# The mLSTM gates' projection and their side work, moved behind the Fourier projection and spread over the jobs of the attention's values

## The chip, the cores and the metric

The kernel runs on one core of one Trainium2 chip. The metric is device time in microseconds (us) of one execution, as the median over runs. The engines are TensorE (PE: matmuls, with its weight loads as PEld), VectorE (DVE), ScalarE (ACT), GpSimd (POOL) and SyncE (SP, which here issues nearly all DMAs). In the profile L12 means line 12 of the kernel.

## The reference

The program is a trunk of two layers for 256 latent tokens and 256 context tokens of width 1024. In each layer the tokens are normalised and modulated (adaLN), and one input projection feeds three parallel branches, of which these columns matter here:

```python
u = h @ w_in                 # columns: mLSTM q, k, v, o; 16 gate columns; attention q, k, v; Fourier z; ...
i_f, f_f, i_b, f_b = split(u[gate columns] + gate_b, 4)      # 4 heads, forward and backward in time
b = cumsum(log_sigmoid(f))                                   # running sums and maxima of the mLSTM
m_t = maximum(b + m, max over s <= t of (b_t - b_s + i_s))
yd = differential attention with axial rotary of (dq, dk, dv)
yf = real part of a 2-D Fourier transform of z
```

A merge of the branches, a residual and a SwiGLU feed-forward follow. All is float32. The second layer needs the latent tokens' output only.

## The kernel before

A float32 product is made of three matmuls on operands split into a high and a low part: `proj_t` (L303 on) computes W^T h with the weights stationary, and per chunk of 128 rows of W it issues high x high (L310), high x low (L311) and low x high (L312). `proj_n` (L331 to L333) is the form with the tokens as rows. The weights come as *jobs*, one per block of W. A job is loaded by SP (`wr`, L204, 512 KB; four raw buffers), its high part `wh` is cast by ACT (L214, about 1.05 us), its low part `wl` is made by DVE (L224, about 1.25 us), and then its matmuls run. `run_all` writes the program job by job: it loads 7 jobs ahead and splits 3 ahead. Jobs of `proj_t` have 24 matmuls. A matmul over 512 tokens is issued every 0.23 us, one over 256 every 0.12 us.

Beside the jobs run *sides*: generators (`side(name, gen, steps, jobs)`) that are advanced one step at a time between pieces of the jobs, spread evenly over a stated number of jobs, and finished by `drain(name)`. SP keeps the program's order; the other engines' order is made by the scheduler of the framework from the program's order and the buffers that are free. PSUM has four main banks (`m`, the jobs' results) and four side banks (`p`).

One layer's attention and Fourier part runs, in the program's order, as follows. Four (layer 0) or three (layer 1) dk jobs run inside the opening of the layer, while the tokens are normalised. Then come the rest of the eight dk jobs, eight dq jobs (in layer 1 over the 256 latent tokens alone, like dq's matmuls there), the Fourier projection z (`proj_z`, eight jobs, folded weights: sums of two raw blocks made by DVE and POOL at L790, edges copied by ACT at L792; layer 0's matmuls are L813 to L815, layer 1's L817; at its end 32 or 16 small matmuls, L837), eight dv jobs, and then q, k, v of the mLSTM. Each dk or dq job ends in a rotary evacuation from its bank, four DVE products L1215, one L1216 and a POOL sum L1217. The dv jobs keep all four main banks for four jobs, and evacuate them by copies that DVE (L1362) and ACT share.

The gates' job (`GateJob`) is a `proj_t` job with 16 used columns: POOL clears its raw buffer (L231), SP loads it by four DMAs (L233), ACT casts it, and POOL, not DVE, makes the low part (L222). Its result stays in a side bank. `ml_gates` (L1003 to L1072) is its side work in 18 steps on 36 rows of 512: DVE copies the bank out (L1016, L1019), adds the bias (L1025), forms a log-sigmoid by a polynomial (twelve times L1033), a running sum (L1040) and a running maximum (L1045), copies the results with the backward half reversed (L1055, L1057); then PE transposes them eight times (L1062) and DVE takes the columns out (L1066). The mLSTM, far later, is the first to use them.

Two more sides matter: `adab` and `adac` compute rows of the modulation from w_ada (per step two DMAs of 512 KB at L365, and eight matmuls L372 in four column strips), and `hf` (`fold_h`, L751 to L774) folds the tokens for z on DVE.

Of the kernel before, what the change touches and what calls it, by code (L numbers as in the profile page):

```python
# [26 lines left out]
CQ, CK, CV, CO, CGATE, CDQ, CDK, CDV, CZ, CG = 0, 1024, 2048, 3072, 4096, 4112, 5136, 6160, 7184, 8208  # L27
# [16 lines left out]
def tile_trunk(ctx: ExitStack, tc: tile.TileContext, x, c, cx, c_ctx, w_ada, b_ada, norm_g, w_in, ml_gate_b,  # L44
# [30 lines left out]
    def main_ps():  # L75
        return pm.tile([128, 512], F32, tag="m", name=nm("m"))

    def side_ps():
        return psd.tile([128, 512], F32, tag="s", name=nm("p"))
# [105 lines left out]
    def act_k(acts, k, n0, n1):  # L185
        return acts[0][k // 2][:, k % 2, n0:n1], acts[1][k // 2][:, k % 2, n0:n1]

    def unit_n():
        return upool.tile([128, 4, 256], F32, tag="u4", name=nm("n"))
# [46 lines left out]
    def call(fn):  # L236
        prog.append(("call", fn))

    def side(name, gen, steps, jobs):
        prog.append(("side", name, gen, steps / (4.0 * jobs)))  # L240

    def drain(name):
        prog.append(("drain", name))
# [60 lines left out]
    def proj_t(src, acts, n0, evac, cls=Job):  # L304

        def run(job):
            ps = side_ps() if cls is GateJob else main_ps()
            for k in range(KB):
                ah, al = act_k(acts(), k, n0, NT)
                T.matmul(ps[:, n0:], lhsT=job.hi[:, k, :], rhs=ah, start=(k == 0), stop=False)  # L310
                T.matmul(ps[:, n0:], lhsT=job.hi[:, k, :], rhs=al, start=False, stop=False)  # L311
                T.matmul(ps[:, n0:], lhsT=job.lo[:, k, :], rhs=ah, start=False, stop=(k == KB - 1))  # L312
                if k == KB - 1:
                    evac(ps)
                if k % 2:
                    yield
        prog.append(cls(src, KB, 128, run))

    def proj_n(src, nk, acts, tbs, evac):

        st = {}

        def mk(kt):
            def run(job):
                if kt == 0:
                    st.update({tb: main_ps() for tb in tbs})
                for tb in tbs:
                    for j in range(2):
                        k = 2 * kt + j
                        ah, al = act_k(acts(), k, tb * 128, tb * 128 + 128)  # L330
                        T.matmul(st[tb], lhsT=ah, rhs=job.hi[:, j, :], start=(k == 0), stop=False)  # L331
                        T.matmul(st[tb], lhsT=ah, rhs=job.lo[:, j, :], start=False, stop=False)  # L332
                        T.matmul(st[tb], lhsT=al, rhs=job.hi[:, j, :], start=False, stop=(k == nk - 1))  # L333
                    if kt == nk // 2 - 1:
                        evac(tb, st[tb])
                    yield
            return run
        for kt in range(nk // 2):
            prog.append(Job(src[kt * 256:kt * 256 + 256, :], 2, 512, mk(kt)))
# [994 lines left out]
    def plan(l, xget, fin, bd1, bd2, bdn):  # L1334
# [6 lines left out]
        W = w_in[l]  # L1341
        vc = {n: vcol[:, 32 * l + o:32 * l + o + 8] for n, o in VROW.items()}
        st = {"yd": ([], []), "ym": ([], []), "q": [], "k": [], "v": [], "dq": [], "dk": [], "dv": [],
              "ys": [], "yy": ([], []), "us": ([], []), "ox": []}
# [14 lines left out]
        h = lambda: bd1().h  # L1359
# [17 lines left out]
        def proj_tt(key, c0, nn0, rot=False, b0=0):  # L1377
            for b in range(b0, 8):
                proj_t(W[:, c0 + b * 128:c0 + b * 128 + 128], h, nn0, evac_t(key, nn0, b, rot))

        def proj_nn(key, c0, tt, f):
            for g in range(2):
                def evac(tb, ps, g=g):
                    if tb == tt[0]:
                        st[key] += [unit_n(), unit_n()]
                    for j in range(2):
                        f(st[key][2 * g + j][:, tb, :], ps[:, j * 256:j * 256 + 256], j)
                proj_n(W[:, c0 + g * 512:c0 + g * 512 + 512], KB, h, tt, evac)
# [61 lines left out]
            opening_jobs(bd1, specs, parts)  # L1450
        else:
            first_jobs(bd1, specs)
        proj_t(W[:, CGATE:CGATE + 16], h, 0, lambda ps: st.__setitem__("gps", ps), GateJob)
        call(start)
        side("gates", lambda: ml_gates(l, st["gps"], st), 18, 10)
        side("adab", ada[1].steps, 10, 10)
        proj_tt("dk", CDK, 0, True, nop)
        side("hf", lambda: fold_h(h(), len(segs), hf, st), 12 if l == 0 else 8, 7 * nT // 4)
        proj_tt("dq", CDQ, n0, True)
        drain("gates")  # L1460
        drain("adab")
        drain("hf")
        proj_z(l, W, len(segs), hf, st)
        side("adac", ada[2].steps, 10, 8)
        proj_nn("dv", CDV, ALL, cp)
        drain("adac")
        qjobs = 8 * nT // 4
        side("da", lambda: diff_attn(l, st, tbs), (8 * nT + 4) * 3, qjobs + 15)
# [134 lines left out]
    ctx.enter_context(tc.manual_schedule(engines={mybir.EngineType.SP}))  # L1603
    call(begin)
    plan(0, None, fin, bd[0], bd[1], bd[2])
    plan(1, lambda: fin[0], fin, bd[2], bd[3], bd[4])
    run_all()

# [55 lines left out]
```

## Time and profile before

| | before |
|---|---|
| median of 3 runs | 2001.8 us (1996.95 to 2003.03) |
| the profiled execution | 1996.54 us, span 1994.5 us, mean granted clock 0.987 |
| PE busy | 1930.8 us, 97% of the span |
| DVE busy | 1192.4 us, 60% |
| ACT busy | 783.6 us, 39% |
| POOL busy | 148.1 us, 7% |

Times are in us from the span's start. [...] A row of the timeline gives an instruction's start and duration, and in brackets the idle time before it with what ended it. Matmuls are pipelined, so a row's duration (0.39 us for 512 columns) is longer than the distance to the next.

### The profile page before, as it was taken

To read this page: it belongs to the slowest core of one execution; us is meant where nothing else is said; L and a number is where in the kernel's file an instruction comes from. 1 tells how busy PE (TensorE), PEld (TensorE's weight loads), DVE (VectorE), ACT (ScalarE), POOL (GpSimd) and SP (SyncE) were. 2 spreads that over 40 slices of the span, in tenths; PEclk is the share of its full clock that TensorE was granted. 3 is DMA by queue.
4 is the path that set the end of the run, shared out by engine and by line. 5 is a ranking of instruction groups with operands and counts; after the bars stand their busy time and mean duration, and the time that the engine had idled before them with its cause. 6 is when DMAs were issued, how large, how long until landed. Compare 5 with 4: busy or idle time off the path is not lost.

```text
span 1994.5 us, 27678 instructions
## 1 busy us (share of the span) xinstructions
PE 1930.8 (97%) x10504; PEld 1591.5 (80%) x10504; DVE 1192.4 (60%) x2592; ACT 783.6 (39%) x1466; POOL 148.1 (7%) x164
## 2 busy tenths in 40 slices
PE   6999999999999999999999999989999999989998
PEld 4768687888777778888777888776878978879996
DVE  4895488852476457653333235982984486476655
ACT  3223376632344223352222224322773354235443
POOL 0240000000000110000000000250100010000000
PEclk8999999999999999999999999999999999899999
DMA  9547522224321333434443332668322654465663
GB/s 292 171 138 222 194 64 60 58 92 120 116 74 54 95 86 115 159 106 137 148 137 95 117 95 44 213 204 283 96 64 83 184 171 143 119 187 158 182 198 130
DMA packets 339895, 269.49 MB, mean 135 GB/s; under 512 B 17233, under 2 KB 296145, under 8 KB 339762
## 3 DMA queue, kind: packets, MB, share of 16 engines
q1 hardware_dynamic: 339040, 265.09, 43.9%
q10 hardware_dynamic: 722, 2.62, 0.3%
q8 instruction: 83, 1.36, 0.3%
q14 instruction: 50, 0.41, 0.1%
HBM read 264.73 MB, written 7.11 MB: 136 GB/s over the span
## 4 chain that ended last, share of the span: by engine, by line
PE 76%; DVE 14%; ACT 4%; DMA 3%; issue 2%; SPq 0%; POOL 0%; DVEq 0%; ACTq 0%; POOLq 0%
PE m L310 12%; PE m L312 12%; PE m L311 12%; PE m L331 6%; PE m L333 6%; PE m L332 6%; DVE wl L224 3%; PE p L1152 2%; DVE t L1215 2%; PE m L568 2%; PE m L566 2%; PE m L567 2%; PE p L372 1%; PE p L1116 1%; PE m L681 1%
## 5 line engine op out<-in xcount | busy, mean ns | idle before, releaser
L224 DVE TENSOR_TENSOR wl<-wr,wh 128x1024 fp32r<-128x1024 f32 x336 | 418.7, 1249 | 446.2 <-ACT wh L214 444.6
L214 ACT CAST wh<-wr 128x1024 fp32r<-128x1024 f32 x336 | 351.6, 1049 | 687.1 <-issue 265.3
L310 PE MATMUL m<-u,wh 128*128 128x512 f32 (+1 forms) x1752 | 616.3, 352 | 1.7 <-ACT wh L214 1.7
L312 PE MATMUL m<-u,wl 128*128 128x512 f32 (+1 forms) x1752 | 604.0, 345 | 1.6 <-DVE wl L224 1.6
L311 PE MATMUL m<-u,wh 128*128 128x512 f32 (+1 forms) x1752 | 602.9, 344 | 0.0
L310 PEld LDWEIGHTS m<-u,wh 128*128 128x128 f32 x1752 | 334.2, 191 | 63.2 <-issue 13.8
L312 PEld LDWEIGHTS m<-u,wl 128*128 128x128 f32 x1752 | 333.8, 191 | 41.5 <-DVE wl L224 2.7
L311 PEld LDWEIGHTS m<-u,wh 128*128 128x128 f32 x1752 | 334.1, 191 | 38.8 <-issue 3.2
L331 PE MATMUL m<-wh,u 128*128 128x512 f32 x532 | 216.3, 407 | 0.0
L333 PE MATMUL m<-wh,u 128*128 128x512 f32 x532 | 208.4, 392 | 0.0
L332 PE MATMUL m<-wl,u 128*128 128x512 f32 x532 | 207.9, 391 | 0.0
L331 PEld LDWEIGHTS m<-wh,u 128*128 128x128 f32 x532 | 100.0, 188 | 32.5 <-issue 13.8
L333 PEld LDWEIGHTS m<-wh,u 128*128 128x128 f32 x532 | 99.9, 188 | 21.4 <-issue 0.2
L332 PEld LDWEIGHTS m<-wl,u 128*128 128x128 f32 x532 | 100.1, 188 | 20.6 <-issue 1.7
L1258 ACT ACTIVATE u<-p,s 128x512 f32<-128x512 f32 (+1 forms) x96 | 59.4, 618 | 39.9 <-DVE s L1257 37.7
L566 PE MATMUL m<-wh,u 128*128 128x512 f32 x180 | 70.2, 390 | 0.0
L568 PE MATMUL m<-wh,u 128*128 128x512 f32 x180 | 70.0, 389 | 0.0
L567 PE MATMUL m<-wl,u 128*128 128x512 f32 x180 | 70.0, 389 | 0.0
L1517 DVE SCALAR_TENSOR_TENSOR t<-t,m 128x512 f32<-128x512 f32 (+1 forms) x44 | 24.4, 554 | 62.7 <-PE m L312 62.1
L1255 DVE TENSOR_REDUCE s<-p 128x1 f32<-128x512 f32 (+1 forms) x96 | 57.1, 595 | 7.3 <-PE p L1253 7.1
L1215 DVE TENSOR_TENSOR t<-m,cst 32x256 f32<-32x256 f32 x128 | 53.8, 420 | 6.6 <-ACT u L1373 4.3
L1217 POOL TENSOR_TENSOR u<-u,t 128x256 f32<-128x256 f32 x32 | 43.6, 1363 | 153.2 <-DVE u L1216 134.2
(288 smaller groups left out, 2523.1 us busy)
## 6 DMA issues: line engine op xcount, KB each, us to landing
wr<-in_w_in_dram SPq DMA_DIRECT2D x176, 512.0 KB
wr<-in_w_ffn_in_dram SPq DMA_DIRECT2D x88, 512.0 KB
u<-in_w_ada_dram SPq DMA_DIRECT2D x80, 512.0 KB
wr<-in_w_ffn_out_dram SPq DMA_DIRECT2D x44, 512.0 KB
u<-in_w_ada_dram SPq DMA_DIRECT2D x32, 256.0 KB
wr<-in_w_br_da_dram SPq DMA_DIRECT2D x16, 512.0 KB
wr<-in_w_br_ml_dram SPq DMA_DIRECT2D x16, 512.0 KB
wr<-in_w_out_dram SPq DMA_DIRECT2D x16, 512.0 KB
```

Of the source, the lines that this page charges most:

```text
L214: S.copy(self.hi, self.raw)
L224: V.tensor_tensor(out=self.lo, in0=raw, in1=self.hi, op=ALU.subtract)
L310: T.matmul(ps[:, n0:], lhsT=job.hi[:, k, :], rhs=ah, start=(k == 0), stop=False)
L311: T.matmul(ps[:, n0:], lhsT=job.hi[:, k, :], rhs=al, start=False, stop=False)
L312: T.matmul(ps[:, n0:], lhsT=job.lo[:, k, :], rhs=ah, start=False, stop=(k == KB - 1))
L331: T.matmul(st[tb], lhsT=ah, rhs=job.hi[:, j, :], start=(k == 0), stop=False)
L332: T.matmul(st[tb], lhsT=ah, rhs=job.lo[:, j, :], start=False, stop=False)
L333: T.matmul(st[tb], lhsT=al, rhs=job.hi[:, j, :], start=False, stop=(k == nk - 1))
L566: T.matmul(ps[tb], lhsT=ah, rhs=job.hi[:, j, :], start=(k == 0), stop=False)
L567: T.matmul(ps[tb], lhsT=ah, rhs=job.lo[:, j, :], start=False, stop=False)
L568: T.matmul(ps[tb], lhsT=al, rhs=job.hi[:, j, :], start=False, stop=(k == nk - 1))
L1215: V.tensor_tensor(out=r[32 * a:32 * a + 32, :], in0=ps[src, 256:512], in1=ropes[src, :], op=ALU.mult)
```

## The change

Three lines move. The gates' projection and its side leave their place between the opening and the dk jobs and stand behind `proj_z`; the side is spread over the 8 dv jobs in place of the 10 jobs of dk and dq, and it is finished after dv in place of after dq. No computation is added or left out.

```diff
@@ -1450,19 +1450,19 @@
             first_jobs(bd1, specs)
-        proj_t(W[:, CGATE:CGATE + 16], h, 0, lambda ps: st.__setitem__("gps", ps), GateJob)
         call(start)
-        side("gates", lambda: ml_gates(l, st["gps"], st), 18, 10)
         side("adab", ada[1].steps, 10, 10)
         proj_tt("dk", CDK, 0, True, nop)
         side("hf", lambda: fold_h(h(), len(segs), hf, st), 12 if l == 0 else 8, 7 * nT // 4)
         proj_tt("dq", CDQ, n0, True)
-        drain("gates")
         drain("adab")
         drain("hf")
         proj_z(l, W, len(segs), hf, st)
+        proj_t(W[:, CGATE:CGATE + 16], h, 0, lambda ps: st.__setitem__("gps", ps), GateJob)
+        side("gates", lambda: ml_gates(l, st["gps"], st), 18, 8)
         side("adac", ada[2].steps, 10, 8)
         proj_nn("dv", CDV, ALL, cp)
+        drain("gates")
         drain("adac")
```

On PE in layer 0, the transposes of the gates stand before the change among the matmuls of dq (`m_1114` and `m_1188` are banks of dq jobs, `p_714` is adab's):

```order
L312 MATMUL m_1114<-u_235,wl_929 128x512
L310 MATMUL m_1114<-u_235,wh_928 128x512
L311 MATMUL m_1114<-u_239,wh_928 128x512
L312 MATMUL m_1114<-u_235,wl_929 128x512
L1062 MATMUL p_1160<-cst,u_685 128x36 x4
L372 MATMUL p_714<-u_1034,s_79 32x512 x2
L372 MATMUL p_714<-u_1036,s_79 32x512 x2
L310 MATMUL m_1188<-u_232,wh_987 128x512
L311 MATMUL m_1188<-u_236,wh_987 128x512
```

After the change the same engine has them behind the first block of the eighth dv job (`m_1778` and `m_1779` are banks of dv, `p_1625` is adac's):

```order
L331 MATMUL m_1778<-wh_1772,u_235 128x512
L332 MATMUL m_1778<-wl_1773,u_235 128x512
L333 MATMUL m_1778<-wh_1772,u_239 128x512
L1062 MATMUL p_1923<-cst,u_1594 128x36 x8
L372 MATMUL p_1625<-u_1843,s_79 32x512 x2
L372 MATMUL p_1625<-u_1845,s_79 32x512 x2
L331 MATMUL m_1779<-wh_1772,u_235 128x512
```

The eight transposes have moved some 470 rows of PE down, and they are now in one piece. On DVE at the end of layer 0's opening, before the change the rotary products of the first dk job (`m_287`) follow the opening's last work:

```order
L515 TENSOR_SCALAR t_516<-p_477,as_90,as_91 128x256 x2
L521 TENSOR_TENSOR u_239<-t_516,u_235 128x256 x2
L1215 TENSOR_TENSOR t_543<-m_287,cst 32x256 x4
L1216 TENSOR_TENSOR u_541<-m_287,cst 128x256
L224 TENSOR_TENSOR wl_553<-wr_275,wh_552 128x1024
```

After the change (the same bank is `m_283`) a weight split stands ahead of them, that of the fifth dk job, which is now the first job behind the opening:

```order
L515 TENSOR_SCALAR t_512<-p_473,as_90,as_91 128x256 x2
L521 TENSOR_TENSOR u_239<-t_512,u_235 128x256 x2
L224 TENSOR_TENSOR wl_534<-wr_269,wh_533 128x1024
L1215 TENSOR_TENSOR t_539<-m_283,cst 32x256 x4
L1216 TENSOR_TENSOR u_537<-m_283,cst 128x256
L224 TENSOR_TENSOR wl_549<-wr_271,wh_548 128x1024
```

So one split has moved ahead of the first rotary. On DVE in the middle of dv of layer 0, before the change the four copies out of the main banks stand next to each other:

```order
L224 TENSOR_TENSOR wl_1749<-wr_1581,wh_1748 128x1024
L1362 COPY n_1760<-m_1639 128x256
L1362 COPY n_1760<-m_1640 128x256
L1362 COPY n_1760<-m_1641 128x256
L1362 COPY n_1760<-m_1642 128x256
L224 TENSOR_TENSOR wl_1805<-wr_1637,wh_1804 128x1024
```

After the change the end of the gates' polynomial, the running sum (L1040) and the running maximum (L1045) stand between them:

```order
L1362 COPY n_1723<-m_1572 128x256
L1033 SCALAR_TENSOR_TENSOR u_1617<-u_1617,u_1616 36x512
L1037 SCALAR_TENSOR_TENSOR u_1617<-u_1616,u_1617 36x512
L1362 COPY n_1723<-m_1573 128x256
L1040 SCALAR_TENSOR_TENSOR u_1594<-t_1595,u_1617 36x512
L1362 COPY n_1723<-m_1574 128x256
L1044 SCALAR_TENSOR_TENSOR u_1617<-u_1594,gb_1588 36x512
L1045 SCALAR_TENSOR_TENSOR u_1616<-u_1617 36x512
L1362 COPY n_1723<-m_1575 128x256
```

So the copies that give the banks back to PE now have five of the gates' instructions between the first and the last of them.

## Rows read from the trace of the kernel before

**Rows 1.** The page: busy time, share of the span and instructions of each engine.

```profile
PE 1930.8 (97%) x10504; PEld 1591.5 (80%) x10504; DVE 1192.4 (60%) x2592; ACT 783.6 (39%) x1466; POOL 148.1 (7%) x164
```

**Rows 2.** PE's waits between 60 and 240 us (layer 0, from the opening's end through dv): what waits, for what, the total, the number and the longest.

```profile
PE p L1062 <- DVE u L1057: 4.1, 2, 3.8
PE m L815 <- DVE wl L224: 2.3, 1, 2.3
PE p L312 <- POOL wl L222: 0.9, 1, 0.9
```

**Rows 3.** The same between 1245 and 1400 us (layer 1), and, from the timeline of PE, the wait for the gates' low part there.

```profile
PE p L1062 <- DVE u L1057: 3.5, 1, 3.5
PE m L817 <- DVE u L790: 1.4, 1, 1.4
PE p L372 <- DMA u<-in_w_ada_dram: 1.3, 3, 0.8
1250.75 0.50 PE L312 MATMUL p<-u,wl 128*128 128x512 f32 x1 [0.85 <-POOL wl L222]
```

**Rows 4.** Stretches of layer 0: length, busy time and count of PE, PEld, DVE, ACT and POOL, then granted clock, DMA share and GB/s. 127 to 138 is the stretch of the transposes in dq, 154 to 182 z, 182 to 235 dv.

```profile
127.00:138.00 11.00, 6.86 (x30) 3.45 (x29) 10.75 (x23) 2.03 (x8) 0.82 (x1) 0.84 0.62 192
154.00:182.00 28.00, 25.70 (x226) 24.35 (x225) 22.84 (x23) 14.18 (x27) 2.85 (x3) 1.00 0.56 156
182.00:235.00 53.00, 53.00 (x256) 36.50 (x256) 14.77 (x20) 13.66 (x22) 2.42 (x3) 1.00 0.78 268
```

**Rows 5.** The timeline of PE around the transposes of layer 0.

```profile
131.95 0.28 PE L1062 MATMUL p<-cst,u 36*128 36x36 f32 x2 [3.78 <-DVE u L1057]
...
137.73 0.40 PE L310 MATMUL m<-u,wh 128*128 128x512 f32 x1
137.97 0.39 PE L311 MATMUL m<-u,wh 128*128 128x512 f32 x1
```

**Rows 6.** The timelines of PE: the first and the last of the four pieces into which two steps of adab are cut in layer 0, a step in one piece, and the first and the last of the seven pieces of three cut steps in layer 1.

```profile
87.10 1.05 PE L372 MATMUL p<-u,s 128*32 128x512 f32 x4
...
95.45 1.05 PE L372 MATMUL p<-u,s 128*32 128x512 f32 x4
101.43 1.06 PE L372 MATMUL p<-u,s 128*32 128x512 f32 x8
...
1298.69 1.05 PE L372 MATMUL p<-u,s 128*32 128x512 f32 x4 [0.82 <-DMA u<-in_w_ada_dram]
...
1321.17 1.05 PE L372 MATMUL p<-u,s 128*32 128x512 f32 x4
```

**Rows 7.** The end of layer 0's opening: the gates' first matmul on PE, and the timeline of DVE.

```profile
61.44 0.39 PE L310 MATMUL p<-u,wh 128*128 128x512 f32 x1
60.77 1.72 DVE L1215 TENSOR_TENSOR t<-m,cst 32x256 f32<-32x256 f32 x4 [2.63 <-ACT u L1373]
62.51 0.42 DVE L1216 TENSOR_TENSOR u<-m,cst 128x256 f32<-128x256 f32 x1
62.85 1.22 DVE L224 TENSOR_TENSOR wl<-wr,wh 128x1024 fp32r<-128x1024 f32 x1
```

**Rows 8.** The timeline of PE behind the wait for the transposes of layer 1.

```profile
1314.90 0.41 PE L310 MATMUL m<-u,wh 128*128 128x256 f32 x1
1315.11 0.41 PE L311 MATMUL m<-u,wh 128*128 128x256 f32 x1
...
1317.74 0.28 PE L312 MATMUL m<-u,wl 128*128 128x256 f32 x1
1317.86 0.28 PE L310 MATMUL m<-u,wh 128*128 128x256 f32 x1
```

**Rows 9.** Stretches of layer 1, columns as in rows 4: dk and the first half of dq, and the rest of dq up to the transposes.

```profile
1256.00:1298.00 42.00, 41.87 (x233) 31.64 (x231) 38.37 (x62) 10.34 (x16) 9.57 (x6) 1.00 0.76 244
1298.00:1314.00 16.00, 11.41 (x72) 7.45 (x72) 15.81 (x34) 2.97 (x9) 8.09 (x7) 1.00 0.66 221
```

**Rows 10.** The side work of the gates on DVE between 61 and 182 us by line: count, busy us and mean ns.

```profile
L1033 DVE SCALAR_TENSOR_TENSOR u<-u,u 36x512 f32<-36x512 f32 x12 | 8.7, 726 | 0.3
L1040 DVE TENSOR_TENSOR_SCAN u<-t,u 36x512 f32<-36x512 f32 x1 | 3.4, 3416 | 0.0
L1044 DVE SCALAR_TENSOR_TENSOR u<-u,gb 36x512 f32<-36x512 f32 x1 | 1.2, 1221 | 0.0
```

**Rows 11.** The timeline of DVE in the middle of layer 0's dv.

```profile
201.95 0.42 DVE L1362 COPY n<-m 128x256 f32<-128x256 f32 x1
...
206.39 0.42 DVE L1362 COPY n<-m 128x256 f32<-128x256 f32 x1 [0.94 <-PE m L333]
```

**Rows 12.** The tile of the gates' weights over both layers (engine, operation, count: shortest, median and longest ns), and the issue of its four DMAs in each layer (start, duration).

```profile
L222 POOL TENSOR_TENSOR wl<-wg,wh x2: 2375/2384/2392, 60.5 to 1248.3; 128x1024 fp32r<-128x1024 f32 x2
36.38 6.37 SPq L233 DMA_DIRECT2D wg<-in_w_in_dram  x4
1203.88 2.24 SPq L233 DMA_DIRECT2D wg<-in_w_in_dram  x4
```

**Rows 13.** DVE and POOL in layer 1's z.

```profile
1323.18 1.21 DVE L790 TENSOR_TENSOR u<-wr,wr 128x1016 f32<-128x1016 f32 x1
1332.87 3.12 DVE L790 TENSOR_TENSOR u<-wr,wr 128x1016 f32<-128x1016 f32 x1
1332.57 2.34 POOL L790 TENSOR_TENSOR u<-wr,wr 128x1016 f32<-128x1016 f32 x1 [1.23 <-DMA wr<-in_w_in_dram]
```

## The prediction

> **What bounds the kernel now.** The busy times come first: PE works 97% of the span, DVE 60% [rows 1], so a gain has to come from PE's idle time, from a low clock, or from matmuls that PE makes less well. The list of PE's waits over the stretch that the change touches comes second. From the opening's end to the end of dv PE waits 7.3 us in layer 0 [rows 2] and 7.1 us in layer 1 [rows 3]. The longest wait in each layer is that of the transposes L1062 for the last copies L1057 of the gates' side. The stretches show why: from 127 to 138 us DVE is busy 10.75 of 11 us, since rotary, weight splits, the folds for z and the gates all want it, while in dv it is busy 14.77 of 53 [rows 4]. So the gates' chain ends late where DVE is full, and PE, which takes its queue in order, stands at the transposes with matmuls behind them that need nothing from them. A second loss follows: behind the wait the granted clock of that stretch is 0.84 and the distances of matmuls are nearly doubled until 137.73 us.
>
> **The change, part by part.** Durations are from the profiled execution (1996.54 us, 5.3 us under the median of 2001.8); the sum is made against it. No matmul and no DVE work is added, and the 24 matmuls of the gates' job cost the same at either place.
>
> *Transposes, layer 0.* From the start of the wait (131.95 - 3.78 = 128.17) to 137.73, where the distance is 0.24 again [rows 5], lie 9.56 us. By the order they hold six matmuls (6 x 0.23 = 1.4), one adab step (1.06, [rows 6]) and eight transposes. These have no row at full clock; with 0.28 for a pair at the start [rows 5] they lie between 0 and 1.1 us, and I take 0.5. They are paid again in dv. So 9.56 - 1.4 - 1.06 - 0.5 = 6.6 us go.
>
> *Transposes, layer 1.* The wait is 3.5 us [rows 3]; then 13 matmuls come at 0.21 us in place of 0.12 [rows 8], 1.2 us. Together 4.7 us go.
>
> *Cut steps of adab.* A step of eight matmuls L372 takes 1.06 us, a piece of four 1.05 [rows 6]: a cut costs a whole step. Before the change two steps are cut in layer 0 into four pieces, and three in layer 1 into seven; by the order after it one in each, into two. That is one piece fewer than before in layer 0, 1.06, and three fewer in layer 1, 3.1.
>
> *The opening.* The wait of 0.9 us for POOL's low part goes in both layers [rows 2, 3]. What is late next is the main bank of the fifth dk job. In layer 0 all four banks are taken by the opening's jobs; the first comes free when DVE has finished its rotary, and by the order a weight split now stands ahead of it. DVE could start about 60.5 (its rotary waited for ACT until 60.77): 60.5 + 1.22 + 1.72 + 0.42 = 63.9 [rows 7]. PE was through with the opening at about 61.4 [rows 7], so it waits 2.5 us. Without the split ahead it would be 1.5 us, with DVE starting a us later 3.5; I take 2.5, a net loss of 1.6. In layer 1 only three banks are taken, and the job waits for its own low part behind two rotaries: about 1.4 us in place of 0.9, a loss of 0.5.
>
> *z.* In layer 0 PE waits 2.3 us for a low part L224 that DVE makes late, in layer 1 1.4 us for a fold L790 [rows 2, 3]. DVE comes to z with the gates' backlog gone (L1033 and L1040 alone are 12.1 us, [rows 10]), so in layer 0 I take all of 2.3; in layer 1, where z's own folds and the rotaries are still as dense, half, 0.7. The bounds are nothing and all of it.
>
> *dq of layer 1.* DVE was busy 38.37 of 42 and 15.81 of 16 us [rows 9]. Without the gates it is still close behind PE: a dq job has a rotary (2.14), a split (1.22, [rows 7]) and its share of the folds, against 24 x 0.12 + 1.06 = 3.9 us of PE. I take 1 us of new waits (bounds 0 and 3). The waits for w_ada (1.3 us, [rows 3]) need not go, as the same bytes are now wanted in less time; I take 0.6 (bounds 0 and 1.3).
>
> *dv.* Here the gates' chain now sits. DVE has the room, but the order puts five of its instructions between the four copies that free the main banks. Before, the copies start between 201.95 and 206.39 [rows 11]. Now 0.73 + 1.22 + 3.42 + 1.22 + 1.22 (L1037 and L1045 as long as L1044, [rows 10]) and four copies of 0.42 end at about 201.95 + 9.5 = 211.4. PE wants the fourth bank again one adac step and three blocks of six matmuls later, 206.39 + 1.06 + 3 x 1.37 = 211.6. The cover is just used up, and the rest of the chain with its splits fills about 17 of the 20 us ahead of the first copy, so it may come late. I take 1 us in each layer (bounds 0 and 4). The transposes themselves stand in the eighth dv job, some 10 us behind the chain's end.
>
> *The gates' weights.* Their load is now seven jobs ahead of a place behind z, on SP between the loads of dv. What is queued behind it on SP are dv's weights and adac's, and behind its cast on ACT the evacuations of z. In layer 1, where z has only 15 us of PE's time, POOL by my estimate from the order (a last rotary, a fold, the clearing) has cleared the buffer about 4.5 us into z, the DMAs are issued in 2.24 us, and with landing, cast and POOL's 2.38 [rows 12] the low part is there at about 13: nothing. If the issue takes 6.37 as in layer 0's opening [rows 12], it is there at 17 and costs about 2.
>
> The sum: layer 0: 6.6 + 1.06 - 1.6 + 2.3 - 1 = 7.4; layer 1: 4.7 + 3.1 - 0.5 + 0.7 - 1 + 0.6 - 1 = 6.6. Together 14 us less: 1996.5 - 14 = 1982.5 for a profiled execution, and by the same ratio a median of 1987.8, say 1988.
>
> [...] Row: after waits of 3.8 us the clock was low (0.84), after the 2.3 us in z the stretch kept 1.00 [rows 4]. [...]
>
> [...] Row: a fold L790 on DVE takes 1.21 us alone and 3.12 while POOL has its own fold of 2.34 us running [rows 13]. [...] The gates' split on POOL now lies beside dv's splits, which may so take 2 us longer; they are made three jobs ahead, and the sum stays.
>
> **The rivals.**
>
> *The wait moves into dv.* If the chain on DVE is some 4 us late, PE stands at the fourth bank instead of at the transposes, and the clock falls there as it did before. For it speak the scan of 3.4 us between the copies and a cover of nothing; against it 38 us of idle DVE time in dv. Price: in each layer some 4 us of wait and 2.4 of slow matmuls in place of my 1, so 14 - 2 x 5.4 = 3 us gained: about 1999.
>
> *DVE stays the bound, and the opening costs the clock.* Then layer 1's dq loses 3 us, z's waits stay (3.0 of my sum), and the opening loses 2 to 3 more: 14 - 2 - 3 - 2.5 = 6.5 gained: 1995.
>
> *SP falls behind (slower).* SP issues in order. The gates' four DMAs wait for POOL's clearing, which stands behind z's folds on POOL; adac's and dv's loads stand behind. If that holds the queue for more than the lead of about 9 us that an adac load has, each of the eight steps per layer waits, as w_ada did in layer 1 up to 0.8 us [rows 3]. It decides from there on: 16 steps x 1.3 us = 21 us against a gain of 14: about 2009. Against it: dv's DMA share of 0.78 [rows 4] leaves room to catch up.
>
> *More than the sum.* All unknown costs at their good ends (the opening of layer 0 at 1.5, no new wait in dq and dv, all of the waits for w_ada and in z) give 9.4 + 10.5 = 20 us: 1982; the forecast's middle and this lie close together, and a time below 1980 would be a gain that I have not seen.
>
> **How the numbers follow.** The forecast (7 to 18 us less) has 0.62, more than that 0.06, the wait in dv 0.16, DVE's bound with the clock 0.10, SP 0.06. A measurement of this kernel can tell about 0.3%, 6 us, from no change. Faster: 0.62 + 0.06 + half of 0.10 + a little of the wait in dv = 0.75; slower 0.07; the same 0.18. The forecast's own range is 1984 to 1995. To hold the time 8 times in 10 it reaches from below the good ends to the wait in dv: 1979 to 2000.
>
> **What would show it.** Right: no wait of L1062 in either layer and a granted clock of 1.00 through dq; z of layer 0 starting near 141 us (it started near 154, of which 5.5 are the gates' job); one wait of 2 to 3 us at the opening's end for a rotary; dv of 53 to 54 us. Wrong: a PE wait behind L1362 in the middle of dv, or for L222 or L372 there; DVE full in layer 1's dq with PE waiting for banks; a clock below 1.00 behind the opening. If dv is longer by more than 6 us in each layer, the change has only moved the hole.

## The result, and the profile after

The changed kernel takes 1988.0 us in the median of 4 runs (1986.34 to 1988.74), the kernel before 2002.2 in the median of 4 (1996.95 to 2003.03). The ratio is 0.9937, with a 95% interval of 0.9918 to 0.9956. A second comparison, with 6 runs against 17, gave 0.9948 (0.9933 to 0.9964), 1989.6 us against 2001.1. The profiled execution took 1987.44 us, 9.1 less than that of before.

The page of the changed kernel answers to [rows 1]:

```profile
span 1985.8 us, 27699 instructions
PE 1926.1 (97%) x10504; PEld 1590.9 (80%) x10504; DVE 1192.9 (60%) x2592; ACT 783.3 (39%) x1466; POOL 141.7 (7%) x164
```

The busy shares are what they were, so the page does not show where the time came from. PE's waits between 60 and 240 us (layer 0) do; they answer to [rows 2]:

```profile
PE m L310 <- DVE u L1216: 2.5, 1, 2.5
PE m L815 <- DVE wl L224: 1.9, 2, 1.7
```

The waits at the transposes L1062 and for POOL's low part are gone. The new one at the opening's end is the rotary of 2.5 us, and the wait in z is there nearly as before. Between 1235 and 1400 us (layer 1, [rows 3]):

```profile
PE m L817 <- DVE u L790: 1.4, 2, 1.2
PE m L312 <- DVE wl L224: 1.0, 1, 1.0
PE p L312 <- POOL wl L222: 0.5, 1, 0.5
```

The stretches of layer 0, with the columns of [rows 4]: the new wait, dk and dq, z, dv.

```profile
61.30:64.40 3.10, 0.63 (x4) 0.24 (x2) 3.02 (x7) 3.10 (x6) 0.04 (x1) 1.00 0.39 94
64.40:143.30 78.90, 78.90 (x356) 56.30 (x357) 67.15 (x119) 20.23 (x42) 24.30 (x17) 0.98 0.62 197
143.30:171.40 28.10, 26.11 (x226) 24.42 (x224) 23.16 (x24) 13.37 (x24) 7.55 (x5) 1.00 0.54 134
176.90:233.50 56.60, 56.60 (x277) 39.47 (x276) 37.85 (x59) 16.55 (x25) 5.09 (x7) 1.00 0.71 234
```

The same work of dk and dq in the kernel before, with 4.3 us of idle PE:

```profile
68.12:153.94 85.82, 81.49 (x364) 56.29 (x363) 83.03 (x151) 21.66 (x41) 27.69 (x18) 0.98 0.56 179
```

PE has no idle time at all in dk and dq, nor in dv, and DVE is busy 67.15 of 78.90 us in dk and dq, where before it was busy 83.03 of 85.82. After the change the 0.98 of dk and dq (the granted clock, TensorE's as a share of full speed) comes from one slow piece right behind the new wait, in which matmuls are 0.43 us apart in place of 0.23 (a granted clock of 0.56 from 65.6 to 69.5 us): the stretch in two parts, and PE's rows at its start.

```profile
64.40:70.00 5.60, 5.60 (x18) 4.44 (x19) 5.45 (x10) 0.29 (x1) 3.19 (x2) 0.70 0.51 139
70.00:143.30 73.30, 73.30 (x340) 51.86 (x339) 61.70 (x109) 19.93 (x41) 21.11 (x15) 1.00 0.63 202
64.37 0.47 PE L310 MATMUL m<-u,wh 128*128 128x512 f32 x1 [2.47 <-DVE u L1216]
...
65.60 0.58 PE L312 MATMUL m<-u,wl 128*128 128x512 f32 x1
...
66.41 0.63 PE L311 MATMUL m<-u,wh 128*128 128x512 f32 x1
...
69.48 0.39 PE L310 MATMUL m<-u,wh 128*128 128x512 f32 x1
```

From 65.60 to 69.48 lie ten distances of matmuls, which at 0.23 us each would be 2.3 us and are 3.9: the low clock behind the wait costs 1.6 us. The second trace of the changed kernel has the same wait, 2.5 us, and the same slow piece behind it (0.78 from 58.8 to 66.1 us, the wait included). The eight transposes come in one piece in dv, without a wait, in 0.6 us of PE's time:

```profile
223.76 0.69 PE L1062 MATMUL p<-cst,u 36*128 36x36 f32 x8
```

In the middle of dv, where the prediction saw the cover just used up, DVE does this (it answers to [rows 11]):

```profile
197.13 0.42 DVE L1362 COPY n<-m 128x256 f32<-128x256 f32 x1
197.48 0.67 DVE L1033 SCALAR_TENSOR_TENSOR u<-u,u 36x512 f32<-36x512 f32 x1
198.18 0.68 DVE L1037 SCALAR_TENSOR_TENSOR u<-u,u 36x512 f32<-36x512 f32 x1
...
199.13 1.21 DVE L1040 TENSOR_TENSOR_SCAN u<-t,u 36x512 f32<-36x512 f32 x1
...
202.48 0.39 DVE L1362 COPY n<-m 128x256 f32<-128x256 f32 x1
```

The running sum takes 1.21 us and not 3.4 [rows 10], so the fourth copy is done at 202.9, some 4 us before PE wants the bank.

The two traces can be cut at the same instructions, and this is the finest measure that the case has: layer 0 from the last matmul of the opening (L681) to the first of the mLSTM's attention behind dv (L1252); layer 1's body, from its opening's last L650 to its first L1252; and the tail from there to the last matmul. The starts of these matmuls in PE's timeline give, in us:

| trace | layer 0 | layer 1 body | tail |
|---|---|---|---|
| before | 177.0 | 150.7 | 585.9 |
| after | 172.2 | 142.0 | 590.6 |
| difference | -4.8 | -8.7 | +4.7 |

What remains, between the two layers' parts and in the openings, is near zero in this pair of traces. So the change gains 13.5 us up to the end of dv in layer 1, and almost 5 of them are lost again behind it.

### The profile page after: what moved, and what is told of

Read it like the earlier page. It is cut to its first block, busy times and chain, and to the rows that moved or that the text cites. A ratio compares the mean times of both kernels' runs of the same rounds, so it can differ in the third digit from the quotient of the medians.

```text
span 1985.8 us, 27699 instructions
## 1 busy us (share of the span) xinstructions
PE 1926.1 (97%) x10504; PEld 1590.9 (80%) x10504; DVE 1192.9 (60%) x2592; ACT 783.3 (39%) x1466; POOL 141.7 (7%) x164
## 4 chain that ended last, share of the span: by engine, by line
PE 78%; DVE 11%; DMA 4%; ACT 4%; issue 2%; POOL 0%; SPq 0%; DVEq 0%; ACTq 0%; POOLq 0%
PE m L310 13%; PE m L312 13%; PE m L311 13%; PE m L331 6%; PE m L333 6%; PE m L332 6%; DVE wl L224 2%; PE p L1152 2%; PE m L568 2%; PE m L567 2%; PE p L372 2%; PE m L566 2%; PE p L1116 1%; DMA wr<-in_w_in_dram 1%; PE m L681 1%
```

## The experiments

Each trace of an experiment was cut in the same way; the table comes at the end of this section.

**The same two programs again.** No edit.

> The changed kernel once more, in another execution. Theory A (the gain made up to the end of dv in both layers, 14.7 us in the first trace, belongs to the change; what was lost again behind it, 1.6 us behind the feed-forward of layer 0, 1.5 in the mLSTM and 3.8 in the last merge of layer 1, is chance of one execution): the same marks up to the end of dv within 0.5 us, and the three later losses gone or of another size. Theory B (the later losses follow from the change): all three come back at the same places within 0.5 us each. Ratio to the kernel before 0.992 to 0.995.

> The kernel before once more, in another execution and against itself. Theory A (the first trace of before was a lucky execution behind dv: 1.5 us less in layer 0's feed-forward than every other trace so far, and 1 to 4 us less in the last merge of layer 1): up to the end of dv the marks of either layer stand as in the first trace within 1 us of their layer's start, and behind it this trace is 2 to 5 us longer, near 1999 to 2001. Theory B (the losses behind dv belong to the changed kernel): this trace is as the first within 1 us throughout. Ratio 1.00.

Measured: the changed kernel 1989.6 us, layer 0 172.2, layer 1's body 142.4, tail 587.9. The kernel before: 1997.0 us in this run of 12 executions, with a ratio to itself of 0.9984 (0.9974 to 0.9995), layer 0 177.1, body 152.7, tail 582.6. Layer 0 repeats to 0.1 us, layer 1's body to 2. What lies between the layers' parts does not always: 1010.9 and 1012.5 us in the two traces of before, 1010.7 and 1015.8 in those of after. Nor does the tail: the wait of 3.1 us for L949 that the first trace of after has in the last merge was 1.3 in the second. Neither theory holds as it was written: the later losses are not the same in the two traces of after, but the second trace of before did not get longer either. And a ratio of 0.9984 for a program against itself says that this kernel's comparisons are good to about 0.2%.

**Only the transposes moved.** The chain of the gates' side stays in dk and dq; its last part, L1062 and what follows, stands in the seventh dv job.

```diff
-        pt = side_ps()
+        st["gt"] = (gi, grow, R)
+
+    def ml_cols(l, st):
+        gi, grow, R = st["gt"]
+        pt = side_ps()
...
+        call(lambda: later(24, lambda: ml_cols(l, st)))
         proj_nn("dv", CDV, ALL, cp)
```

> The kernel before, with nothing moved but the eight transposes and what follows them, which now stand in the seventh dv job; the job, the polynomial, the sums and the copies stay in dk and dq. Theory A (the loss is PE standing at the transposes, and the low clock behind it): the waits for L1057 go, 6 to 6.6 us in layer 0 and 4 to 5 in layer 1; the steps of adab stay cut (two in layer 0, two pieces-pairs fewer or none in layer 1 by the order), so 2 to 4 us less gain than the changed kernel up to the end of dv. Rival (DVE's load is what counts, and PE would stand at the next thing that DVE owes it, a rotary's bank or a low part): new waits of 3 us or more in dq, and a gain up to the end of dv under 6 us.

Measured: ratio 1.0002 (0.9988 to 1.0015); layer 0 177.7, body 151.7. PE's waits in layer 0 of this kernel:

```profile
PE m L814 <- DVE u L774: 3.7, 1, 3.7
PE m L813 <- ACT u L773: 2.5, 1, 2.5
PE p L312 <- POOL wl L222: 0.9, 1, 0.9
PE m L815 <- DVE wl L224: 0.8, 1, 0.8
```

The wait for L1057 is gone and, counted from the opening's end, z starts 7.1 us earlier than before; then PE stands in z for the last folds (L774 and the cast L773 for it), and by dv the 7.1 us are lost again. Theory A falls: PE standing at the transposes was not the loss but the place where it showed. PE had to wait for DVE somewhere before dv, and the transposes came first.

**Less work for DVE, nothing moved.** The polynomial keeps 4 of its 12 terms.

```diff
         for i, cc in enumerate(lp[-2::-1]):
-            V.scalar_tensor_tensor(out=acc, in0=acc, scalar=cc, in1=e, op0=ALU.add, op1=ALU.mult)
+            if i < 4:
+                V.scalar_tensor_tensor(out=acc, in0=acc, scalar=cc, in1=e, op0=ALU.add, op1=ALU.mult)
```

> The kernel before with the polynomial of the gates cut to 4 of its 12 terms at the same steps (the log-sigmoid is then not computed as the reference has it), so 5.8 us less of DVE's work in each layer's dk and dq and nothing moved. Theory A (the transposes wait because DVE's chain is late by its own load): the waits of 3.8 and 3.5 us at the transposes shrink to 0 to 1 and the clock stays at 1.00, a gain of 5 to 6.6 us in layer 0 and 4 to 5 in layer 1. Rival (the chain is late because its steps are handed out late, not because DVE is full): the waits stay above 2.5 us.

Measured: layer 0 172.8, 4.2 us less than before for 5.8 us less of DVE's work, with the transposes where they were. The wait at them is gone in layer 0; a wait of 1.9 us for the last fold, L774, came up in z in its place. The ratio of this comparison is 0.9946 (0.9926 to 0.9967), but it rests on 4 executions (1986.53 to 1993.45 us) of which the profiled one is the longest, so the median's 12 us are more than the trace can account for. In layer 1 the wait stayed (L1063 and L1058 are the lines L1062 and L1057 here):

```profile
PE p L1063 <- DVE u L1058: 3.3, 1, 3.3
PE p L372 <- DMA u<-in_w_ada_dram: 2.5, 2, 1.6
```

Its stretches of layer 1 up to that wait, with the columns of [rows 4]:

```profile
1251.00:1293.00 42.00, 42.00 (x226) 31.58 (x225) 37.26 (x62) 10.45 (x16) 7.19 (x7) 1.00 0.73 229
1293.00:1309.00 16.00, 11.36 (x84) 8.19 (x82) 15.76 (x32) 2.97 (x9) 8.40 (x6) 1.00 0.86 294
```

DVE is still busy 15.76 of 16 us in front of the wait: 5.8 us less were not enough in layer 1, where dq has the same rotaries but matmuls of half the length (0.12 us apart in place of 0.23). The body was 150.2, between 0.5 and 2.5 us less than before. So for layer 1 it is the job in front (below) that shows what the side work costs.

**Half of the chain behind.** The gates' side is spread from dk to the end of dv.

```diff
-        side("gates", lambda: ml_gates(l, st["gps"], st), 18, 10)
+        side("gates", lambda: ml_gates(l, st["gps"], st), 18, 26)
...
-        drain("gates")
...
         proj_nn("dv", CDV, ALL, cp)
+        drain("gates")
```

> The kernel before with the gates' side spread from dk to the end of dv (26 jobs) and finished there: by the order 8 of the 12 polynomial instructions of layer 0 stay in dk and dq, 4 lie in z, and all that follows, about 11 us of DVE, lies in dv with the transposes. Theory C (DVE is the bound over dk, dq and z taken together, and PE waits wherever DVE's lateness shows first): between the kernel before and the changed one, 2 to 4.5 of the 4.8 us of layer 0 up to the end of dv, with what waits there are in z and not in dq. Rival (only the transposes' place counts): then cols_late would have gained as much; or (any of the chain in front costs all): no gain, with waits of 5 us or more in z as in cols_late.

Measured: ratio 0.9994 (0.9979 to 1.0009); layer 0 176.5, body 153.1. PE's waits of layer 0:

```profile
PE m L814 <- DVE u L774: 2.6, 1, 2.6
PE m L813 <- ACT u L773: 2.2, 1, 2.2
PE m L815 <- DVE wl L224: 1.8, 1, 1.8
```

Again z starts early (7.4 us, counted from the opening's end) and again PE waits in z, 6.6 us. The dose that I forecast (2 to 4.5 of the 4.8 us) did not come; 0.5 did, which is the second rival of the expectation. The four polynomial instructions that lie in z share DVE with z's folds and splits. What counts is that DVE is free of the chain when z comes: in this kernel's z DVE is busy 31.90 of 32.30 us, as full as dq was.

**The job in front, its side in dv.** As changed, but the gates' job stands between the opening and dk.

```diff
+        proj_t(W[:, CGATE:CGATE + 16], h, 0, lambda ps: st.__setitem__("gps", ps), GateJob)
         call(start)
...
         proj_z(l, W, len(segs), hf, st)
-        proj_t(W[:, CGATE:CGATE + 16], h, 0, lambda ps: st.__setitem__("gps", ps), GateJob)
         side("gates", lambda: ml_gates(l, st["gps"], st), 18, 8)
```

> The gates' job stays where it was before the change, between the opening and dk; only its side work moves to dv. Theory A (the side work on DVE in dk and dq is the whole loss, and moving the job itself costs 1.6 us at the opening of layer 0, where a split on DVE now delays the rotary that PE waits for): the wait for L1216 of 2.5 us at 64 us becomes one of about 0.9 for POOL's low part, dk to dv otherwise as in the changed kernel, 1 to 2 us faster than it in layer 0 and within 1 us in layer 1. Rival (the job's own move is part of the gain, since its loads no longer compete at the opening): not faster than the changed kernel in either layer.

Measured: layer 0 171.1, 1.1 us less than the changed kernel; body 144.6, 2.2 to 2.6 more, where theory A allowed 1, with waits for w_ada of 1.3 us that the changed kernel does not have; ratio 0.9948 (0.9930 to 0.9967), the same time. The 1.1 us hide two larger numbers. From the opening's end to z this kernel takes 84.1 us, of which 5.5 are the gates' job, and the changed kernel 81.8: 3.2 us, twice the 1.6 of theory A, since with the wait of 2.5 us the slow piece behind it is gone too. But z takes 28.1 us in place of 26.1, as here the clock fell behind the wait of 1.7 us that both kernels have in z:

```profile
158.00:163.00 5.00, 4.94 (x28) 4.94 (x29) 3.83 (x5) 2.08 (x5) 0.00 (x0) 0.66 0.56 186
```

So the move of the side alone brings the gain, in both layers; the job's own move costs some 3 us at layer 0's opening, and in the median it is neutral.

**The opening's price by itself.** As changed; the low part of layer 0's fifth dk job is made on POOL.

```diff
+    class PoolJob(Job):
+        pool = True
...
+                       PoolJob if l == 0 and key == "dk" and b == b0 else Job)
```

> The changed kernel with the low part of layer 0's fifth dk job made on POOL in place of DVE, so that no split stands ahead of the first rotary on DVE. Theory A (the wait of 2.5 us at the opening's end is split plus rotary): it falls by the split's 1.2 us to 1.2 to 1.5, and layer 0 gains 1 to 1.3 us, no more than 0.1% of the time. Rival (the rotary is late for another reason, or POOL's 2.4 us are waited for instead): the wait stays between 2 and 3 us.

Measured: the rotary's wait fell from 2.5 to 1.5 us, as forecast. (The line numbers of this kernel are 3 higher.)

```profile
PE m L313 <- DVE u L1219: 1.5, 1, 1.5
PE p L155 <- DVE s L152: 1.1, 1, 1.1
```

The clock stayed up behind this shorter wait, and it fell later, in z:

```profile
63.00:70.00 7.00, 6.56 (x29) 5.46 (x30) 6.80 (x14) 2.75 (x6) 3.59 (x3) 1.00 0.70 184
157.50:162.50 5.00, 5.00 (x31) 5.00 (x30) 3.67 (x4) 2.27 (x3) 0.39 (x1) 0.66 0.85 151
```

The wait is 1.0 us shorter and the slow piece of 1.6 us is gone, but a small wait for L152, 0.2 us in the kernel before and none in the changed one, is now 1.1: from the opening's end to z 1.4 us are gained. z is 1.5 us longer with its low clock, and layer 0 stayed at 172.4. The ratio is 0.9941 (0.9924 to 0.9958): nothing gained that the median can show.

**The cover in dv.** As changed, each polynomial instruction three times.

```diff
-            V.scalar_tensor_tensor(out=acc, in0=acc, scalar=cc, in1=e, op0=ALU.add, op1=ALU.mult)
+            for _ in range(3):
+                V.scalar_tensor_tensor(out=acc, in0=acc, scalar=cc, in1=e, op0=ALU.add, op1=ALU.mult)
```

> The changed kernel with each of the 12 polynomial instructions issued three times (the log-sigmoid is then not the reference's), 24 more of 0.71 us, 17 us of DVE's work more in each layer's dv. In the first trace the fourth copy out of the main banks ended at 202.9, and PE wanted the bank at about 206.6, so the cover is some 4 us. Theory A (dv has a cover of 4 us at the banks, then PE waits): PE waits behind L1362 in the middle of dv, in all 2 to 8 us in each layer, as part of the 17 lies ahead of the first copy and is made up in DVE's idle time, and the transposes are late by less than 3 us. Rival (dv has room for any such work): no wait over 0.5 us, and the time of the changed kernel.

Measured: ratio 0.9989 (0.9971 to 1.0008), layer 0 179.4, body 149.2: with 17 us more of DVE's work in dv the gain is gone in the median. The ten executions lie apart: four took 1991.2 to 1992.2 us at a mean clock of 0.988 or 0.989, six 2000.9 to 2004.6 at 0.983 or 0.984, and the trace is of one of the six. In it there was no wait at the banks; the scheduler had laid the copies ahead of the rest of the chain. The wait was at the transposes, 2.1 us in each layer, and the clock fell behind it, with a matmul's row at 0.63 us in place of 0.39 (PE's timeline of layer 0):

```profile
223.81 0.39 PE L332 MATMUL m<-wl,u 128*128 128x512 f32 x1
226.29 0.29 PE L1063 MATMUL p<-cst,u 36*128 36x36 f32 x2 [2.09 <-DVE u L1058]
...
230.75 0.63 PE L333 MATMUL m<-wh,u 128*128 128x512 f32 x1
...
234.23 0.39 PE L311 MATMUL m<-u,wh 128*128 128x512 f32 x1
```

The wait of 2.1 us, one of 0.5 at the first matmul behind dv, and 4.6 of slow work between them (the low clock, with the transposes strewn among the matmuls) make the 7.2 us by which layer 0 is longer than in the changed kernel. So dv's room for the chain is real and has an end. What the four shorter executions did not pay is not shown, as none of them was traced.

**One layer at a time.** The change in layer 0 alone, and in layer 1 alone, by conditions on l at the five moved lines, as here for the first:

```diff
+        if l == 1:
+            proj_t(W[:, CGATE:CGATE + 16], h, 0, lambda ps: st.__setitem__("gps", ps), GateJob)
```

> The change in layer 0 alone; layer 1 as before. Theory A (the layers' gains are separate, and what is given back behind layer 1's dv follows from layer 1's change): 4.8 us from the opening's end to q in layer 0, layer 1's body (from the opening's end to q) 150 to 153 us as before, the tail behind it 583 to 586 us; time about 5 us under the kernel before. Theory B (the tail grows by 3 to 5 us whenever anything ahead of it moves): tail 587 to 591, and nothing left of the gain.

> The change in layer 1 alone; layer 0 as before. Layer 0 177.0 us from the opening's end to q as in both traces of before; layer 1's body 142 to 143 us in place of 151 to 153; theory A: the tail 587 to 591 us as in the traces of the changed kernel, so 5 of the 9 us are given back, and the time 4 to 6 us under the kernel before; theory B: the same tail as l0_only's.

Measured, layer 0 alone: 173.8, body 151.1, tail 590.5, ratio 0.9991 (0.9975 to 1.0007). Layer 1 alone: 177.0, body 142.1, tail 588.6, ratio 0.9971 (0.9956 to 0.9986). The layers' gains are separate. The tail is long in both, also where layer 1 is built as before, so its 3 to 8 us are not a consequence of moving layer 1's gates: theory A of the tail falls. Theory B's numbers came, a tail of 587 to 591 and nothing left of the gain, though not what would cause them. Layer 0's 173.8 is 1.5 more than the changed kernel's with the same waits; here the clock was 0.94 in z, and there it was 1.00:

```profile
138.50:166.00 27.50, 25.51 (x185) 24.38 (x184) 22.47 (x27) 13.02 (x27) 8.08 (x6) 0.94 0.47 112
```

The same stretch in the second trace of after:

```profile
138.60:166.10 27.50, 25.49 (x198) 24.37 (x197) 23.33 (x27) 13.14 (x26) 8.07 (x6) 1.00 0.48 112
```

**The wait that stayed in z.** As changed; layer 0's odd folds go to POOL, and in the second kernel layer 0's gates' job also goes back to the front.

```diff
-            (G if self.odd and not self.do_split else V).tensor_tensor(out=self.raw[:, :, 1:128], in0=a[:, :, 1:128], in1=b[:, :, 127:0:-1],
+            (G if self.odd else V).tensor_tensor(out=self.raw[:, :, 1:128], in0=a[:, :, 1:128], in1=b[:, :, 127:0:-1],
```

> The changed kernel with the odd folds of layer 0's z made on POOL, as in layer 1, in place of DVE: four of L790's 1.2 us go from DVE in z. Theory A (the wait of 1.9 us that stayed in z is z's own chain on DVE, three folds ahead of three splits, and never was the gates' backlog): the waits for L224 in z fall to 0 to 0.6 and layer 0 from the opening's end to q from 172.2 to 170.5 to 171. Rival (the loads of z come late, or POOL's folds of 2.3 us and their contention with DVE take the place): a wait of 1.5 us or more stays, for L224 or for POOL's L790.

> z_pool with the gates' job of layer 0 put back in front of dk (its side work stays in dv, layer 1 as changed): the two remedies together. Theory A: 1.2 us less again, 169.3 to 170 us in layer 0, some 3 us under the changed kernel, 0.15% and hardly to be told from it by its median. Rival: the two share one wait, 171 us or more.

Measured: layer 0 179.3 and 176.5, ratios 0.9978 (0.9963 to 0.9993) and 0.9955 (0.9936 to 0.9974). The remedy made it worse: the wait in z rose from 1.9 to 5.8 us. DVE and POOL in z of the first of the two:

```profile
154.38 5.04 DVE L790 TENSOR_TENSOR u<-wr,wr 128x1016 f32<-128x1016 f32 x2
159.34 6.76 DVE L224 TENSOR_TENSOR wl<-u,wh 128x1024 fp32r<-128x1024 f32 x4
...
155.01 6.60 POOL L790 TENSOR_TENSOR u<-wr,wr 128x1016 f32<-128x1016 f32 x2
```

Two folds on DVE take 5.04 us beside POOL's folds, and POOL's two 6.60, where one took 1.21 and 2.34 [rows 13]. Nothing was won by the second hand. Together the two remedies are 2.8 us better than the folds on POOL alone, so putting the job in front does help beside it.

No version beats the changed kernel by more than the comparisons can tell.

| kernel | layer 0 | layer 1 body | tail |
|---|---|---|---|
| before, second trace | 177.1 | 152.7 | 582.6 |
| after, second trace | 172.2 | 142.4 | 587.9 |
| only the transposes moved | 177.7 | 151.7 | 587.3 |
| short polynomial | 172.8 | 150.2 | 586.1 |
| half of the chain behind | 176.5 | 153.1 | 586.5 |
| job in front | 171.1 | 144.6 | 590.8 |
| fifth dk job's low part on POOL | 172.4 | 142.1 | 590.1 |
| polynomial three times | 179.4 | 149.2 | 589.6 |
| layer 0 alone | 173.8 | 151.1 | 590.5 |
| layer 1 alone | 177.0 | 142.1 | 588.6 |
| odd folds on POOL | 179.3 | 142.1 | 588.5 |
| the same, job in front | 176.5 | 143.1 | 590.2 |

## Why the prediction was right, and where it was not

The time came out as forecast, 1988.0 us, with a ratio of 0.9937. The sum up to the end of dv was 14 us and the traces show 13.5. But its parts were not all right: two of them failed in layer 0, z and the clock behind the opening, layer 1 made up for them, and the tail was not in the sum.

*What held.* The reading that DVE is full in dk and dq and has room in dv (busy 14.77 of 53 us before [rows 4], 37.85 of 56.60 after), and that the gates' chain is what makes PE wait there, is what the experiments confirm: work taken from DVE gains in layer 0 with nothing moved (short polynomial, 4.2 us), the side's move gains without the job's in both layers (job in front), and PE's waiting place moved without DVE's work gains nothing (only the transposes moved). The wait at layer 0's opening was right: 2.5 us, of which the split is 1.0. No wait came up in dv, and the gates' weights came in time in layer 0.

*The clock behind the opening: a term put at nothing.* The sum took nothing for a low clock behind the new wait of 2.5 us. The clock fell there in both traces of the changed kernel, in the first to 0.70 from 64.4 to 70.0 us, and cost 1.6 us; the job's move costs 3.1 to 3.2 us at the opening and not 1.6. This is one of the signs of being wrong that the prediction named, a clock below 1.00 behind the opening, and one half of its second rival. No run shows the 2 to 3 us that this rival takes for it; in their place the trace shows 1.6. The row on which a clock kept behind the wait could rest, 1.00 after 2.3 us in z [rows 4], was a single case.

*Transposes and cut steps, layer 0.* Forecast 6.6 + 1.06 = 7.7; dk and dq went from 85.8 us (68.12 to 153.94) to 78.9 (64.37 to 143.28), 6.9 less, and the 78.9 hold the slow piece of 1.6, so the term itself gave 8.5. It is near in size, but its working was not the cause: I priced the wait, its slow clock and a cut, as if the transposes alone had to go. The kernel with only the transposes moved shows that these 7 us come back in z as long as the chain is on DVE.

*z, layer 0: the step that failed.* "DVE comes to z with the gates' backlog gone ... so in layer 0 I take all of 2.3". z took 25.97 us before (153.94 to 179.91) and 26.1 after. DVE did not come to z earlier. Its rows around dq's last rotary (L1216), before:

```profile
159.99 0.42 DVE L1216 TENSOR_TENSOR u<-m,cst 128x256 f32<-128x256 f32 x1
160.34 4.01 DVE L790 TENSOR_TENSOR u<-wr,wr 128x1016 f32<-128x1016 f32 x3
```

and after:

```profile
151.23 0.42 DVE L1216 TENSOR_TENSOR u<-m,cst 128x256 f32<-128x256 f32 x1
151.57 1.22 DVE L224 TENSOR_TENSOR wl<-u,wh 128x1024 fp32r<-128x1024 f32 x1
152.70 4.00 DVE L790 TENSOR_TENSOR u<-wr,wr 128x1016 f32<-128x1016 f32 x3
```

This part of the rotary starts some 6 us behind z's first matmul before the change and some 8 behind it after. In both kernels three folds in a row follow, and PE's longest wait in z is for the first of the splits behind them: the wait is made by the order of z's own work on DVE, and there was no backlog of the gates to lose. The attempt to shorten z's chain through POOL lengthened it, so this last point rests on the two kernels' traces and not on an experiment that removed the wait.

*Layer 1: under-sized.* Forecast 6.6, measured 8.7. dk and dq with the opening's end gained 10.3 us (78.0 - 5.5 for the gates' job before, 62.2 after) where I had 6.9: the new wait of 1 us that I put into dq did not come, the waits for w_ada went wholly (1.3 in place of 0.6), POOL's wait at the opening was replaced by one of 1.0 in place of 1.4, and 0.85 us of transposes left dq, which the sum left out because they are paid again in dv. z lost 1.1 in place of gaining 0.7, half of it the wait of 0.5 us for the gates' low part that I had priced at nothing.

*dv.* I took 1 us of new waits per layer. There was none; layer 0's dv is 0.4 us longer, the transposes' own time. The five instructions between the copies took 4.5 us in place of the 7.8 that I summed from dq's rows: of those rows L1040 (3.42 us, in dv 1.21) and L1044 (1.22, in dv 0.74) had run beside POOL's work (see the last section), and in dv nothing of POOL's but a clearing of 0.10 us ran beside the five.

*The rivals.* The wait did not move into dv: its cover is 4 us, and only 17 us more of DVE's work brought a wait, at the transposes. SP did not fall behind. Of the second rival the clock at the opening came and layer 0's wait in z stayed; DVE did not stay the bound in layer 1's dq.

*The tail.* Behind layer 1's dv both traces of after are longer than both of before, by 2 to 8 us. The medians of the two kernels differ by 14.2 and 11.5 us, the profiled executions by 9.1. The profiled execution of before was faster than all four runs that it was first compared by, that of after was in the middle of its own, which is why the medians lie further apart than the traces. Two things are seen in the long tails. One is a wait of about 1 us at L1141 that before has in neither trace, but the short polynomial and the half of the chain have it too (0.9 and 1.0 us), and their tails, 586.1 and 586.5, are next to the first of before, 585.9. The other is the wait for L949 in the last merge, here of the changed kernel:

```profile
1748.91 2.06 PE L963 MATMUL m<-u,u 128*128 128x129 f32 x8 [3.12 <-DVE u L949]
```

and of the kernel before:

```profile
1758.58 1.13 PE L963 MATMUL m<-u,u 128*128 128x129 f32 x8 [1.13 <-DVE u L949]
```

The second trace of after has only 1.3 us there. As layer 0's change alone has the long tail too, and PE, DVE and POOL do the same instructions in the same order there as before, it is no term of the moved work. Why most altered builds have a tail of 587 to 591 us, and those two and before do not, stays open. So the agreement of the median with the forecast is in part luck: a failed term in z, a clock put at nothing, an under-sized layer 1, and a tail that I had not counted.

## What to carry to other kernels

Where PE waits in a stretch in which another engine is full, the wait names the place and not the cause: move the waiting instruction alone and the wait appears at the next thing that engine owes. Sum the full engine's work over the whole stretch up to the point where it has room, and move work of that engine across this point, all of it. A duration taken while another engine's work ran beside it can be too long for a place without that work (the running sum: 3.42 us in dq, 1.21 in dv), so the cover there can be better than it says. And a new wait of PE can have a second price: read the granted clock of the few us behind it, since over a long stretch it hardly shows (0.70 over 5.6 us, 0.98 over 78.9).

## What the runs showed of the hardware

A running sum on 36 x 512 elements took 3.42 us in dq of layer 0, while POOL had a sum of 128 x 1024 of its own running (4.18 us there), and 1.21 us in dv. The two lines of the kernel before:

```profile
108.43 4.18 POOL L758 TENSOR_TENSOR u<-u,u 128x1024 f32<-128x1024 f32 x1
110.27 3.42 DVE L1040 TENSOR_TENSOR_SCAN u<-t,u 36x512 f32<-36x512 f32 x1
```

In layer 1's dq, where DVE was just as full but POOL had nothing running, the same sum took 1.22 us:

```profile
1288.49 1.22 DVE L1040 TENSOR_TENSOR_SCAN u<-t,u 36x512 f32<-36x512 f32 x1
```

In z of the kernel with the odd folds on POOL, where both engines fold, DVE's two folds took 5.04 us, about twice their time alone (1.21 us for one, [rows 13]). POOL's took 3.3 us each in place of 2.34, but the 2.34 of [rows 13] was also beside a fold of DVE, so what slowed POOL there is not shown. Nor was every fold of DVE longer beside one of POOL: in the kernel before, the fold of DVE behind those of [rows 13], at 1336.65 us, took 1.22 us, while POOL's beside it took 3.41. What makes the longer ones longer, the traces do not show.

PE's clock does not follow the length of the wait alone. Behind the wait of 2.5 us at the opening's end it was low in the changed kernel (0.70 from 64.4 to 70.0 us, and 0.78 in the second trace from 58.8 to 66.1) and with layer 0 alone (0.81 from 58.7 to 66.0 us; the last two stretches hold the wait too), and the wait of 1.5 us (fifth dk job's low part on POOL) left the clock up, at 1.00. The wait of 2.3 us in z of the kernel before left it up (1.00, [rows 4]), one of 2.09 us in dv was followed by slow work (a row of 0.63 us at 230.75 us, in place of the 0.39 that stood again at 234.23), and of five traces with a wait of 1.7 us at the same place in z three show a slow piece behind it (layer 0 alone with 0.94 over z, job in front and fifth dk job's low part on POOL with 0.66 over 5 us) and the two of the changed kernel do not (1.00 over z). The prediction had a single pair of rows to go by, 0.84 behind a wait of 3.8 us and 1.00 behind one of 2.3; at the opening 2.5 us went with the first of the two. By these runs a wait of some 2 us can cost its own duration alone (2.3 in z), 1.6 us on top of 2.5 (the opening), or, with the transposes among the matmuls, 4.6 on top of 2.1 (dv).
